# Grid attention by pairs of heads: score and value products on alternating halves of the array

## The chip, the cores and the metric

One core of one Trainium2 chip runs the whole kernel. The metric is the device time of one execution in microseconds (us); the kernel before takes 1773.36 us, the median of three runs (1773.16 to 1774.51).

In the rows, PE is the matrix engine (TensorE), PEld its loads of stationary operands, DVE is VectorE, ACT is ScalarE, POOL is GpSimd and SP is the queue that issues DMAs. "L879" is line 879 of the kernel.

## What is computed

One layer of a diffusion backbone: 512 latent tokens of 1024 channels, 256 context tokens. Three mixers (a gated convolution, a gated recurrence, a grid attention) run on one projection of the normalised tokens, are merged by gates and projected; a mixture of 16 experts follows. The change lies in the grid attention alone:

```python
def neighbourhood_attention(q, k, v, kc, vc, rpb):
...
        s_loc = jnp.einsum('bnqhd,bwnkhd->bhnqwk', qr, kr) * scale + bias[None]
        s_loc = jnp.where(in_win[:, :, None, :], s_loc, MASK_VALUE).reshape(...)
        s_ctx = jnp.einsum('bnqhd,blhd->bhnql', qr, kc) * scale
        p = jax.nn.softmax(jnp.concatenate([s_loc, s_ctx], axis=-1), axis=-1)
...
        o = jnp.einsum('bhnqwk,bwnkhd->bnqhd', p_loc, vr) + jnp.einsum('bhnql,blhd->bnqhd', p_ctx, vc)
```

There are 8 heads of width 64. The grid is 8 rows by 64 columns; a block of 16 columns (128 queries) sees 256 keys of the grid and all 256 context keys, so each softmax row has 512 entries.

## The kernel before

The first sub-layer is a stream of projections. Weights come in items of 1 MiB (`load_item`, L332); each is split into a high and a low part by `split_item` (L340): ScalarE casts a quarter (L353), VectorE subtracts it (L354), four quarters per item, spread over the first half of the steps of the item before. `proj` (L433) issues the products of one block of 128 channels: 8 steps of three 512-column matmuls (L440) into a bank `pj`.

Each engine runs its instructions in the order in which the program issues them. That order is written by `weave(fg, bg)` (L167): it issues the foreground steps `fg` one by one and puts the background pieces `bg` between them, evenly by cost. In the stage around the change (L1111) the foreground is the twelve projections of the convolution branch and four of the gates, 128 steps of three matmuls, and three small pieces that transpose the last value rows (`v_rows`, L840); the background is the grid attention.

The attention has 32 units, one per head and block of 16 columns. Two heads share a 128-row tile: head u = 0 lies on partitions 0 to 63, u = 1 on 64 to 127 of `nq`, `nk`, `nkc`. One background piece, `att_slot(n)` (L870), does one step of a pipeline that is four units deep:

- unit n: two score products (L879 grid keys, L880 context keys; 64 rows, 256 columns each) into a bank `hg`; VectorE adds the bias (L883) and takes the negated maximum (L884); ScalarE takes the exponential with the sum (L886);
- unit n − 1: VectorE takes the reciprocal of the sum (L890) and scales the row (L891);
- unit n − 3: four transposes (L896) into the bank `tp`, copied out by ScalarE (L898);
- unit n − 4: four value products (L910, stationary operand 64 columns wide, 128 columns streamed) into half of the partitions of a bank `acc`.

There are two `hg` banks, one `tp` bank, two `acc` banks and three `pj` banks. The operands of the attention are plain fp32, and the trace has two passes (a weight load and a matmul each) for every score and value product; transposes and the projections' matmuls have one. After the stage come the merge of the branches (L985), the output projection, the router and the experts, whose 384 MiB of weights stream through a ring of buffers (`ring_load`, L1017).

Of the kernel before, what the change touches and what calls it, by code (L numbers as in the profile page):

```python
# [10 lines left out]
F32 = mybir.dt.float32  # L11
F32R = mybir.dt.float32r
# [3 lines left out]
ALU = mybir.AluOpType  # L16
# [117 lines left out]
def mixer_moe(ctx: ExitStack, tc: tile.TileContext, a, out):  # L134
# [10 lines left out]
    def bank(tag):  # L145
        return psum.tile([128, 512], F32, tag=tag, name=tag, bufs=pbufs[tag])
# [8 lines left out]
    def g512(dt=F32):  # L155
        return gen.tile([128, 512], dt, tag="g", name="g", bufs=NA_)
# [23 lines left out]

# [1 line left out]
    xt = [[y512() for _ in range(2)] for _ in range(6)]  # L182
# [55 lines left out]

# [1 line left out]
    ssq = small([128, 6, 2], "ssq")  # L240
# [58 lines left out]

# [1 line left out]
    def mod_mm(pm, k, wm):  # L301
# [105 lines left out]

# [1 line left out]
    PASSES = ((0, 0), (0, 1), (1, 0))  # L409

    def use_item(n, blocks):
        """Steps of one streamed item, with the loads and splits of the next ones between them."""
        todo = split_item(n + 1)
        steps = []
        flat = [st for b in blocks for st in b]
        at = {int(p * len(flat) / 6): p for p in range(4)}
        for i, (c, f) in enumerate(flat):
            def g(i=i, f=f):
                if i == 0:
                    load_item(n + 1)  # L420
                    load_item(n + 2)
                f()
                if i in at and at[i] < len(todo):
                    todo[at[i]]()
            steps.append((c, g))
        return steps
# [6 lines left out]
    def proj(n, b, evac, with_ctx=False):  # L433
        """Channels of one block of columns over the tokens; the context follows LAG steps behind."""
        st = {}
# [23 lines left out]

# [1 line left out]
    slabs, mods = {}, {}  # L461
# [47 lines left out]

# [1 line left out]
    hv_t = per.tile([128, 8, 512], F32, tag="acc", name="hv", bufs=1)  # L511
# [33 lines left out]
    class Norms:  # L545
        """Norms over the head widths of several tiles at once: each head has a row of sums."""

# [3 lines left out]
        def sums(self, t, g, kind, cols=slice(0, 512)):  # L551
            """Sums of a tile's squares into row group g; kind 2 halves them, for twice the width."""
            def f():
                if not self.seen:
                    self.p = bank("acc")
                self.left -= 1
                PE.matmul(self.p[32 * g:32 * g + 32], zsel[kind], t(), start=(g not in self.seen), stop=(self.left == 0),
                          skip_group_check=True)
                self.seen.add(g)
            return f  # L560
# [33 lines left out]

# [1 line left out]
    def halves(t, m, lo=0, n=512):  # L596
# [200 lines left out]

# [1 line left out]
    perm_k = lambda t: t.rearrange("p (b r c) -> p r b c", b=8, r=8)  # L799
# [59 lines left out]

# [1 line left out]
    au = [(hp, cb, u) for hp in range(4) for cb in range(4) for u in range(2)]  # L861
    ast = {}
# [6 lines left out]

    def att_slot(n):  # L870
        def f():
            if n < 32:
                hp, cb, u = au[n]
                if n % 8 == 6 and hp < 3:
                    att_load(hp + 1)
                r = slice(64 * u, 64 * u + 64)
                qs = nq[hp][r, 128 * cb:128 * cb + 128]
                ps = bank("hg")
                PE.matmul(ps[:, 0:256], qs, nk[hp][r, 64 * KB0[cb]:64 * KB0[cb] + 256], start=True, stop=True)  # L879
                PE.matmul(ps[:, 256:512], qs, nkc[hp // 2][r, 256 * (hp % 2):256 * (hp % 2) + 256],  # L880
                          start=True, stop=True)
                st_ = gen.tile([128, 4], F32, tag="st", name="st", bufs=4)
                V.tensor_tensor(ps[:, 0:256], ps[:, 0:256], ast["b", hp, BTYPE[cb]][:, u], op=ALU.add)  # L883
                V.tensor_reduce(st_[:, 0:1], ps, axis=AX.X, op=ALU.max, negate=True)  # L884
                p = g512()
                S.activation(p, ps, AF.Exp, bias=st_[:, 0:1], accum_out=st_[:, 1:2])  # L886
                ast["p", n] = (p, st_)
            if 0 <= n - 1 < 32:
                p, st_ = ast["p", n - 1]
                V.reciprocal(st_[:, 2:3], st_[:, 1:2])  # L890
                V.tensor_scalar(p, p, st_[:, 2:3], None, op0=ALU.mult)  # L891
            if 0 <= n - 3 < 32:
                p, _ = ast.pop(("p", n - 3))
                pt = bank("tp")
                for c in range(4):
                    PE.transpose(pt[:, 128 * c:128 * c + 128], p[:, 128 * c:128 * c + 128], ident)  # L896
                pT = g512()
                S.copy(pT, pt)  # L898
                ast["t", n - 3] = pT
            if 0 <= n - 4 < 32:  # L900
                hp, cb, u = au[n - 4]
                pT = ast.pop(("t", n - 4))
                if (n - 4) % 8 == 0:
                    ast["o"] = bank("acc")
                po = ast["o"]
                vs = (nv["lat"][:, KB0[cb]], nv["lat"][:, KB0[cb] + 2], nv["ctx"][:, 0], nv["ctx"][:, 1])
                r = slice(64 * u, 64 * u + 64)
                hc = slice(128 * hp + 64 * u, 128 * hp + 64 * u + 64)
                for c in range(4):
                    PE.matmul(po[r, 128 * cb:128 * cb + 128], vs[c][:, hc], pT[:, 128 * c:128 * c + 128],  # L910
                              start=(c == 0), stop=(c == 3))
                if (n - 4) % 8 == 7:
                    hi, lo = g512(F32R), g512(F32R)
                    S.copy(nat_q(hi), perm_q(po))
                    V.tensor_tensor(nat_q(lo), perm_q(po), nat_q(hi.bitcast(F32)), op=ALU.subtract)
                    yv[2][hp] = (hi, lo)
        return f

# [1 line left out]
    cst = {}  # L920
# [24 lines left out]

# [1 line left out]
    mm = [None] * KT  # L947
# [53 lines left out]

# [1 line left out]
    chunks = []  # L1003
# [31 lines left out]

    # ==== the first sub-layer in program order ====
    for s in range(2):
# [21 lines left out]
    def insert(fg, ops):  # L1059
        """Puts (place, cost, function) between the steps of fg; returns it."""  # L1060
        res, ops = [], sorted(ops, key=lambda o: o[0])
        for i, st in enumerate(fg):
            while ops and ops[0][0] <= i:
                res.append(ops.pop(0)[1:])
            res.append(st)
        return res + [o[1:] for o in ops]
# [43 lines left out]
    fg = insert(fg, [(3 + n, 0.5, f) for n, f in enumerate(v_rows(3))])  # L1110
    weave(fg, [att_slot(n) for n in range(36)])  # L1111
    for n in range(4):
# [14 lines left out]

# [1 line left out]
    ga2, gb2 = mods["ga2"], mods["gb2"]  # L1129
# [94 lines left out]

# [1 line left out]
    wk = ctx.enter_context(tc.tile_pool(name="wk", bufs=2, side="right", reuse_waits="tile"))  # L1226
# [42 lines left out]
    def keep_warm(n):  # L1269
        """Products without a reader, so that the tensor engine's clock stays up while the selection runs."""  # L1270
        for _ in range(n):
            PE.matmul(pm, ident, xn[:, 0, 0:512], start=True, stop=True)
# [15 lines left out]

# [1 line left out]
    xps = {}  # L1290

    def chosen(pr):
        """Steps that gather a pair's rows of two channel tiles each."""
        def first():
# [25 lines left out]

# [1 line left out]
    used = [0]  # L1322
# [49 lines left out]
    def spread(e):  # L1372
        """Weights of an expert's slots over the tokens, slots on partitions, twice."""
        ow = wk.tile([128, 4, 2, CAP], F32, tag="s", name="ow")
# [27 lines left out]
    def down_half(e, h, r):  # L1402
        """The last expert goes by halves of the columns; its even and odd rows meet in the sum over the slots."""
        if r == 0:
# [69 lines left out]
```

## Time and profile before

| What | us |
|---|---|
| median of three runs | 1773.36 |
| span of the profiled execution (first to last instruction) | 1770.6 |
| what lies around the span, against the median | 2.8 |
| PE busy | 1667.7 (94%) |
| DVE busy | 572.1 (32%) |
| ACT busy | 367.7 (21%) |
| chain that ended last | PE 73%, DMA 11%, DVE 5% |

The profiled execution has no separate time beside the runs, so its own time is taken as its span and the 2.8 us around it. "Busy" is an average over stages with different limits: the projections keep PE full, and in the last third the chain also runs through DMAs of expert weights. What a change in one stage is worth has to be read in that stage.

### The profile page before, as it was taken

To read this page: it belongs to the slowest core of one execution; us is meant where nothing else is said; L and a number is where in the kernel's file an instruction comes from. 1 tells how busy PE (TensorE), PEld (TensorE's weight loads), DVE (VectorE), ACT (ScalarE), POOL (GpSimd) and SP (SyncE) were. 2 spreads that over 40 slices of the span, in tenths; PEclk is the share of its full clock that TensorE was granted. 3 is DMA by queue.
4 is the path that set the end of the run, shared out by engine and by line. 5 is a ranking of instruction groups with operands and counts; after the bars stand their busy time and mean duration, and the time that the engine had idled before them with its cause. 6 is when DMAs were issued, how large, how long until landed. Compare 5 with 4: busy or idle time off the path is not lost.

```text
span 1770.6 us, 20476 instructions
## 1 busy us (share of the span) xinstructions
PE 1667.7 (94%) x8382; PEld 949.9 (54%) x8382; DVE 572.1 (32%) x1135; ACT 367.7 (21%) x759; POOL 79.0 (4%) x150
## 2 busy tenths in 40 slices
PE   4999999999999999999999999998998998989988
PEld 2767888777777888896343343342432422424322
DVE  3518776435553443334011211121121121202111
ACT  4414445333334332223000010000000100000000
POOL 0214330000000000000000000000000000000000
PEclk8999999999999999999999999999999999999999
DMA  9860111111111233366999999999999999999997
GB/s 343 283 227 25 50 51 67 48 66 66 66 60 42 92 132 109 137 233 238 401 420 420 420 420 421 420 421 420 420 420 421 420 420 421 420 420 420 421 420 299
DMA packets 131690, 487.77 MB, mean 275 GB/s; under 512 B 8973, under 2 KB 12557, under 8 KB 125709
## 3 DMA queue, kind: packets, MB, share of 16 engines
q1 hardware_dynamic: 131596, 486.47, 69.2%
q8 instruction: 66, 1.08, 0.2%
q14 instruction: 28, 0.22, 0.0%
HBM read 484.34 MB, written 2.10 MB: 275 GB/s over the span
## 4 chain that ended last, share of the span: by engine, by line
PE 73%; DMA 11%; DVE 5%; ACT 1%; issue 1%; SPq 0%; DVEq 0%; ACTq 0%
PE pj L1343 19%; PE pj L440 19%; PE acc L1368 9%; PE hg L1397 5%; PE pj L985 4%; PE hg L1311 3%; PE pj L1175 2%; DMA B<-in_w_down_dram 2%; DMA D<-in_w_down_dram 2%; DMA W<-in_w_up_dram 2%; DMA B<-in_w_up_dram 2%; PE acc L910 2%; DVE acc L1400 2%; PE hg L879 1%; DMA A<-in_w_down_dram 1%; PE tp L896 1%
## 5 line engine op out<-in xcount | busy, mean ns | idle before, releaser
L440 PE MATMUL pj<-A,W 128*128 128x512 f32 x1536 | 400.8, 402 | 2.9 <-ACT W L353 1.9
L440 PEld LDWEIGHTS pj<-A,W 128*128 128x128 f32 x1536 | 276.4, 190 | 73.6 <-issue 20.1
L354 DVE TENSOR_TENSOR W<-W 128x512 fp32r<-128x512 f32 (+1 forms) x184 | 121.4, 686 | 155.4 <-ACT W L353 155.2
L1350 DVE TENSOR_TENSOR s<-s,pj 128x512 f32<-128x512 f32 x32 | 22.0, 688 | 453.7 <-PE pj L1343 367.0
L1343 PE MATMUL pj<-W,xe 128*64 128x512 f32 x688 | 156.5, 599 | 7.8 <-DMA W<-in_w_up_dram 4.4
L1348 ACT ACTIVATE s<-pj 128x512 f32<-128x512 f32 x32 | 19.1, 597 | 567.8 <-PE pj L1343 567.8
L1343 PE MATMUL pj<-A,xe 128*64 128x512 f32 x512 | 118.0, 605 | 5.2 <-DMA A<-in_w_gate_dram 4.2
L1397 PE MATMUL hg<-ye,oht 64*128 64x512 f32 x240 | 100.4, 683 | 16.5 <-DVE acc L1400 16.5
L1343 PEld LDWEIGHTS pj<-W,xe 128*64 128x64 f32 x688 | 47.4, 138 | 110.5 <-issue 86.4
L1343 PE MATMUL pj<-B,xe 128*64 128x512 f32 x432 | 98.5, 596 | 6.6 <-DMA B<-in_w_up_dram 4.4
L353 ACT CAST W<-W 128x512 fp32r<-128x512 f32 (+1 forms) x184 | 103.3, 600 | 0.0
L1400 DVE TENSOR_TENSOR acc<-acc,hg 128x512 f32<-128x512 f32 x120 | 77.7, 684 | 37.1 <-PE hg L1397 37.1
L1343 PEld LDWEIGHTS pj<-A,xe 128*64 128x64 f32 x512 | 35.2, 139 | 81.8 <-issue 66.3
L1397 PEld LDWEIGHTS hg<-ye,oht 64*128 64x128 f32 x240 | 32.7, 193 | 81.8 <-DVE acc L1400 69.6
L1389 DVE TENSOR_TENSOR ye<-mod,acc 64x512 f32<-64x512 f32 x30 | 20.6, 686 | 172.2 <-PE acc L1368 171.7
L1368 PE MATMUL acc<-W,at 128*64 128x512 f32 x320 | 71.7, 595 | 2.1 <-DMA W<-in_w_down_dram 2.1
L1343 PEld LDWEIGHTS pj<-B,xe 128*64 128x64 f32 x432 | 29.5, 137 | 70.0 <-issue 52.9
L1358 ACT COPY at<-tp 128x512 f32<-128x512 f32 x32 | 18.8, 586 | 219.1 <-PE tp L1356 218.6
L440 PEld LDWEIGHTS pj<-C,W 128*128 128x128 f32 x384 | 59.2, 190 | 9.2 <-ACT y L612 0.8
L440 PE MATMUL pj<-C,W 128*128 128x256 f32 x384 | 61.8, 283 | 0.0
L1311 PEld LDWEIGHTS hg<-ot,xn 128*128 128x128 f32 x512 | 57.9, 192 | 2.7 <-issue 2.7
L1311 PE MATMUL hg<-ot,xn 128*128 128x128 f32 x512 | 59.1, 276 | 0.2 <-DVE ot L1297 0.2
(289 smaller groups left out, 1875.1 us busy)
## 6 DMA issues: line engine op xcount, KB each, us to landing
W<-in_w_gate_dram SPq DMA_DIRECT2D x44, 1024.0 KB, 18.1
W<-in_w_up_dram SPq DMA_DIRECT2D x42, 1024.0 KB, 17.7
W<-in_w_down_dram SPq DMA_DIRECT2D x40, 1024.0 KB, 18.0
W<-in_w_in_dram SPq DMA_DIRECT2D x34, 1024.0 KB, 4.8
A<-in_w_gate_dram SPq DMA_DIRECT2D x34, 1024.0 KB, 18.1
B<-in_w_up_dram SPq DMA_DIRECT2D x34, 1024.0 KB, 17.5
B<-in_w_down_dram SPq DMA_DIRECT2D x31, 1024.0 KB, 18.1
A<-in_w_up_dram SPq DMA_DIRECT2D x30, 1024.0 KB, 17.9
```

The costliest lines, as they stand in the source:

```text
L353: S.copy(hi[:, sl], raws[n][:, sl])
L354: V.tensor_tensor(lo[:, sl], raws[n][:, sl], hi[:, sl].bitcast(F32), op=ALU.subtract)
L440: PE.matmul(dst, w[wi][:, k, 128 * b:128 * b + 128], src[xi][:, k], start=(k == 0 and p == 0), stop=(k == KT - 1 and p == 2))
L910: PE.matmul(po[r, 128 * cb:128 * cb + 128], vs[c][:, hc], pT[:, 128 * c:128 * c + 128], start=(c == 0), stop=(c == 3))
L985: PE.matmul(st["p"], wb[wi][:, 4 * br + k], yv[br][k][xi], start=(k == 0 and p == 0), stop=(k == 3 and p == 2))
L1175: PE.matmul(st["p"][:, 256 * u:256 * u + 256], mm[k][mi][:, ts], w[wi][:, k], start=(k == 0 and p == 0), stop=(k == KT - 1 and p == 2))
L1311: PE.matmul(px[:, 128 * k:128 * k + 128], xn[:, i, 128 * kk:128 * kk + 128], ot[:, 128 * i:128 * i + 128], start=(i == 0), stop=(i == 3))
L1343: PE.matmul(pg[64 * u:64 * u + 64], xp[:, kk, 64 * (e % 2):64 * (e % 2) + 64], wt[:, k, 512 * u:512 * u + 512], start=(kk == 0), stop=(kk ...
L1350: V.tensor_tensor(est["s", j], est["s", j], pg, op=ALU.mult)
L1368: PE.matmul(est["y"][64 * u:64 * u + 64], lhs, wt[:, k, 512 * u:512 * u + 512], start=(kk == 0), stop=(kk == 15))
L1397: PE.matmul(pc, oht[64 * u:64 * u + 64, 128 * i:128 * i + 128], ye[64 * u:64 * u + 64], start=True, stop=True)
L1400: V.tensor_tensor(av, av, pc, op=ALU.add)
```

## The change

A background piece no longer holds all four pipeline steps of one unit. The unit becomes a pair of heads (16 pairs), and each pair has four separate pieces, which `weave` spreads: `att_scores(n)`, the transposes of the first head of pair n − 1, the value products of pair n − 2, the transposes of the second head of pair n − 1. Scores are issued as key set by key set, head by head, so that neighbouring products use the two row halves of the array and the two `hg` banks; value products alternate between the two column halves and the two halves of `acc`'s partitions. The scaling (reciprocal and multiplication for both heads) is issued at the head of `att_turn(n, 0)`.

```diff
-    au = [(hp, cb, u) for hp in range(4) for cb in range(4) for u in range(2)]
+    au = [(hp, cb) for hp in range(4) for cb in range(4)]
...
+    def att_scores(n):
...
+            rs = [slice(64 * u, 64 * u + 64) for u in range(2)]
+            ps = [bank("hg") for _ in range(2)]
+            qs = nq[hp][:, 128 * cb:128 * cb + 128]
+            for c, keys in enumerate((nk[hp][:, 64 * KB0[cb]:64 * KB0[cb] + 256],
+                                      nkc[hp // 2][:, 256 * (hp % 2):256 * (hp % 2) + 256])):
+                for u in range(2):
+                    PE.matmul(ps[u][:, 256 * c:256 * c + 256], qs[rs[u]], keys[rs[u]], start=True, stop=True)
+            for u in range(2):
                 st_ = gen.tile([128, 4], F32, tag="st", name="st", bufs=4)
-                V.tensor_tensor(ps[:, 0:256], ps[:, 0:256], ast["b", hp, BTYPE[cb]][:, u], op=ALU.add)
-                V.tensor_reduce(st_[:, 0:1], ps, axis=AX.X, op=ALU.max, negate=True)
+                V.tensor_tensor(ps[u][:, 0:256], ps[u][:, 0:256], ast["b", hp, BTYPE[cb]][:, u], op=ALU.add)
+                V.tensor_reduce(st_[:, 0:1], ps[u], axis=AX.X, op=ALU.max, negate=True)
...
+    def att_scale(n):
+        for u in range(2):
+            p, st_ = ast["p", n, u]
+            V.reciprocal(st_[:, 2:3], st_[:, 1:2])
+            V.tensor_scalar(p, p, st_[:, 2:3], None, op0=ALU.mult)
+
+    def att_turn(n, u):
+        def f():
+            if u == 0:
+                att_scale(n)
+            p, _ = ast["p", n, u]
+            pt = bank("tp")
+            for c in range(4):
+                PE.transpose(pt[:, 128 * c:128 * c + 128], p[:, 128 * c:128 * c + 128], ident)
+            pT = g512()
+            S.copy(pT, pt)
...
+    def att_values(n):
...
+            for c in range(4):
+                for u in range(2):
+                    PE.matmul(po[64 * u:64 * u + 64, 128 * cb:128 * cb + 128],
+                              vs[c][:, 128 * hp + 64 * u:128 * hp + 64 * u + 64],
+                              pT[u][:, 128 * c:128 * c + 128], start=(c == 0), stop=(c == 3))
...
+    att_bg = []
+    for n in range(18):
+        att_bg += [att_scores(n) if n < 16 else None,
+                   att_turn(n - 1, 0) if 0 <= n - 1 < 16 else None,
+                   att_values(n - 2) if 0 <= n - 2 < 16 else None,
+                   att_turn(n - 1, 1) if 0 <= n - 1 < 16 else None]
...
-    weave(fg, [att_slot(n) for n in range(36)])
+    weave(fg, att_bg)
```

PE in the middle of the stage, before (`pj` is a projection's bank, `hg` the scores, `tp` the transposed rows, `acc` the output; `W`, `A` are weights and tokens, `nvl`, `nvc` values of grid and context):

```order
L440 MATMUL pj<-A,W 128x512 x9
L879 MATMUL hg<-g 128x256
L880 MATMUL hg<-g 128x256
L896 MATMUL tp<-ident,g 128x128 x4
L910 MATMUL acc<-g,nvl 64x128 x2
L910 MATMUL acc<-g,nvc 64x128 x2
L440 MATMUL pj<-A,W 128x512 x12
```

PE at the same place, changed:

```order
L881 MATMUL hg<-g 128x256 x4
L440 MATMUL pj<-A,W 128x512 x6
L904 MATMUL tp<-ident,g 128x128 x4
L440 MATMUL pj<-A,W 128x512 x6
L921 MATMUL acc<-g,nvl 64x128 x4
L921 MATMUL acc<-g,nvc 64x128 x4
L440 MATMUL pj<-A,W 128x512 x6
L904 MATMUL tp<-ident,g 128x128 x4
```

Scores of two heads stand together, value products of two heads too, and the transposes stand apart with projections before and behind them. Six projection matmuls lie between the scores of pair n and the first transposes of pair n − 1, in all 15 pairs that have both.

DVE, before, one unit and the start of the next (L883 and L884 bias and maximum, L890 and L891 the scaling, L354 the split of weights):

```order
L883 TENSOR_TENSOR hg<-hg,bias 128x256 [waits PE_49]
L884 TENSOR_REDUCE st<-hg 128x1 [waits DVE_49]
L890 RECIPROCAL st<-st 128x1
L891 TENSOR_SCALAR g<-g,st 128x512 [waits DVE_49]
L354 TENSOR_TENSOR W<-W 128x512 [waits Activation_49] x2
L883 TENSOR_TENSOR hg<-hg,bias 128x256 [waits DMAHW6_49,PE_49]
```

DVE, changed, the pair n = 5 (L884, L885 bias and maximum; L894, L895 the scaling):

```order
L884 TENSOR_TENSOR hg<-hg,bias 128x256 [waits DMAHW6_49,PE_49]
L885 TENSOR_REDUCE st<-hg 128x1 [waits DVE_49]
L884 TENSOR_TENSOR hg<-hg,bias 128x256 [waits PE_49]
L885 TENSOR_REDUCE st<-hg 128x1 [waits DVE_49]
L354 TENSOR_TENSOR W<-W 128x512 [waits Activation_49]
L894 RECIPROCAL st<-st 128x1
L895 TENSOR_SCALAR g<-g,st 128x512 [waits DVE_49]
L894 RECIPROCAL st<-st 128x1
L895 TENSOR_SCALAR g<-g,st 128x512 [waits DVE_49]
```

The scaling of pair n − 1 now stands behind the four score operations of pair n, and in this pair behind a split as well. Between the maxima and the scaling there is nothing in 7 of the 15 pairs; a split in n = 1, 5, 9, 11, 12, 14; the convolution's four operations and a split in n = 2; a gated product, its split and a weight split in n = 13.

ACT, changed, the same pair (L887 exponential, L353 cast of weights, L906 copy of transposed rows):

```order
L887 ACTIVATE g,st<-hg,st 128x512 [waits DVE_49,PE_49,Activation_49] x2
L353 CAST W<-W 128x512
L906 COPY g<-tp 128x512 [waits PE_49]
L541 CAST y<-g 128x512 [waits DVE_49]
L926 CAST g<-acc 128x512 [waits PE_49]
L353 CAST W<-W 128x512
L906 COPY g<-tp 128x512 [waits PE_49]
```

The cast that the split needs stands behind both exponentials of the pair; in n = 1 and n = 14 an evacuation of a projection (L946, L984) stands ahead of the cast too.

## Rows read from the trace of the kernel before

**Rows 1.** Busy time by stretch: us, busy (x instructions) by engine, granted clock, DMA share, GB/s

```profile
394.20:572.60 178.40, 178.40 (x894) 130.31 (x893) 90.92 (x186) 65.04 (x143) 0.00 (x0) 1.00 0.17 58
572.60:740.00 167.40, 167.40 (x735) 137.87 (x736) 63.67 (x104) 52.17 (x101) 9.00 (x7) 1.00 0.32 110
1215.00:1770.00 555.00, 503.76 (x2262) 179.25 (x2260) 96.25 (x174) 33.91 (x61) 0.00 (x0) 0.99 1.01 411
```

**Rows 2.** Timeline of PE, one unit: start, us, engine, line, operation, tile, count

```profile
441.60 0.70 PE L879 MATMUL hg<-g 64*128 64x256 f32 x2
442.14 0.59 PE L880 MATMUL hg<-g 64*128 64x256 f32 x2
442.66 0.66 PE L896 MATMUL tp<-ident,g 128*128 128x128 f32 x4
443.25 0.65 PE L910 MATMUL acc<-g,nvl 128*64 128x128 f32 x4
443.74 0.60 PE L910 MATMUL acc<-g,nvc 128*64 128x128 f32 x4
444.27 3.02 PE L440 MATMUL pj<-A,W 128*128 128x512 f32 x12
447.22 0.48 PE L879 MATMUL hg<-g 64*128 64x256 f32 x1
```

**Rows 3.** Chain of waits, runs of one kind of matmul: start, us, engine, tile, line

```profile
600.24 21.80 PE pj L440 x96
...
922.20 7.16 PE hg L1311 x64
...
938.22 13.73 PE pj L1343 x64
951.95 1.11 PE hg L1397 x4
```

**Rows 4.** Timeline of PE, transposes between projections

```profile
384.64 0.60 PE L849 MATMUL tp<-ident,g 128*128 128x128 f32 x4
385.00 0.71 PE L440 MATMUL pj<-A,W 128*128 128x512 f32 x2
```

**Rows 5.** Timeline of DVE, the same unit as rows 2

```profile
442.77 0.43 DVE L883 TENSOR_TENSOR hg<-hg,bias 128x256 f32<-128x256 f32 x1 [0.40 <-PE hg L880]
443.24 0.69 DVE L884 TENSOR_REDUCE st<-hg 128x1 f32<-128x512 f32 x1
443.84 0.15 DVE L890 RECIPROCAL st<-st 128x1 f32<-128x1 f32 x1
444.03 0.49 DVE L891 TENSOR_SCALAR g<-g,st 128x512 f32<-128x512 f32 x1
...
447.94 0.69 DVE L354 TENSOR_TENSOR W<-W 128x512 fp32r<-128x512 f32 x1
```

**Rows 6.** Timeline of ACT, the same unit

```profile
444.02 0.69 ACT L886 ACTIVATE g<-hg,st 128x512 f32<-128x512 f32 x1 [2.46 <-DVE st L890]
...
444.70 0.58 ACT L898 COPY g<-tp 128x512 f32<-128x512 f32 x1
...
447.21 0.61 ACT L353 CAST W<-W 128x512 fp32r<-128x512 f32 x1
```

**Rows 7.** Groups by line and shape, 394.2 to 572.6 us, the convolution on DVE

```profile
L935 DVE SCALAR_TENSOR_TENSOR g<-g,vecs 128x511 f32<-128x511 f32 x4 | 3.0, 752 | 0.1
```

**Rows 8.** Timeline of PE at two waits: in brackets the idle time and its releaser

```profile
56.55 0.74 PE L529 MATMUL pj<-W,A 128*128 128x256 f32 x4 [1.99 <-DVE W L354]
...
154.89 2.05 PE L711 MATMUL hg<-g 128*128 128x128 f32 x8 [3.12 <-DVE g L712]
```

**Rows 9.** Busy time of PE behind those two waits, granted clock before the DMA share

```profile
56.60:63.00 6.40, 4.77 (x38) 1.00 0.53 190
154.20:161.00 6.80, 6.11 (x23) 0.50 0.43 154
```

**Rows 10.** Line 867, loads of the bias

```profile
DMA to landing us min/median/max: 2.7/5.2/7.1
```

More of the change, by code (lines that the diff above doesn't have):

```diff
@@ L868, in att_load @@
             ast["b", hp, t] = b_
-    def att_slot(n):
+    def att_scores(n):
         def f():
[L872 to L881, printed above, removed]
+            hp, cb = au[n]
+            if cb == 3 and hp < 3:
+                att_load(hp + 1)
+            rs = [slice(64 * u, 64 * u + 64) for u in range(2)]
[6 more added lines that the diff above has]
+            for u in range(2):
@@ L882, in f @@
                 st_ = gen.tile([128, 4], F32, tag="st", name="st", bufs=4)
-                V.tensor_tensor(ps[:, 0:256], ps[:, 0:256], ast["b", hp, BTYPE[cb]][:, u], op=ALU.add)
-                V.tensor_reduce(st_[:, 0:1], ps, axis=AX.X, op=ALU.max, negate=True)
+                V.tensor_tensor(ps[u][:, 0:256], ps[u][:, 0:256], ast["b", hp, BTYPE[cb]][:, u], op=ALU.add)
+                V.tensor_reduce(st_[:, 0:1], ps[u], axis=AX.X, op=ALU.max, negate=True)
                 p = g512()
-                S.activation(p, ps, AF.Exp, bias=st_[:, 0:1], accum_out=st_[:, 1:2])
@@ L887, in f @@
[L887 to L916, printed above, removed]
@@ L917, in att_slot @@
-        return f
+                S.activation(p, ps[u], AF.Exp, bias=st_[:, 0:1], accum_out=st_[:, 1:2])
+                ast["p", n, u] = (p, st_)
+        return f
+    def att_scale(n):
[13 more added lines that the diff above has]
+            S.copy(pT, pt)
+            ast["t", n, u] = pT
+            del ast["p", n, u]
+        return f
@@ new lines, in att_values, with f @@
+    def att_values(n):
+        def f():
+            hp, cb = au[n]
+            pT = [ast.pop(("t", n, u)) for u in range(2)]
+            if cb == 0:
+                ast["o"] = bank("acc")
+            po = ast["o"]
+            vs = (nv["lat"][:, KB0[cb]], nv["lat"][:, KB0[cb] + 2], nv["ctx"][:, 0], nv["ctx"][:, 1])
+            for c in range(4):
[3 more added lines that the diff above has]
+                              pT[u][:, 128 * c:128 * c + 128], start=(c == 0), stop=(c == 3))
+            if cb == 3:
+                hi, lo = g512(F32R), g512(F32R)
+                S.copy(nat_q(hi), perm_q(po))
+                V.tensor_tensor(nat_q(lo), perm_q(po), nat_q(hi.bitcast(F32)), op=ALU.subtract)
+                yv[2][hp] = (hi, lo)
+        return f
@@ L920, in mixer_moe @@
+    att_bg = []
[4 more added lines that the diff above has]
+                   att_turn(n - 1, 1) if 0 <= n - 1 < 16 else None]
+    while att_bg[-1] is None:
+        att_bg.pop()
     cst = {}
```

## The prediction

> **What bounds the kernel now.** First the busy time by stretch [rows 1]. From 394.2 to 572.6 us, the stage that holds the attention, PE is busy for all of its 178.4 us; DVE for 91 and ACT for 65. So TensorE alone sets the length of this stage, and the two engines that evacuate have slack on average. The next stage, to 740 us, is all PE as well. Behind it the experts' weights stream at 411 GB/s, and the last third is bound by that stream; but the stream starts when the buffers of the first sub-layer come free, so a stage that ends x us earlier or later moves all behind it by x. I find nothing behind the stage that would absorb it, and count one for one.
>
> Then one unit on the timeline of PE [rows 2]. From its first score at 441.60 to the next unit's at 447.22 it takes 5.62 us, without an idle gap. A projection matmul in a long run costs 21.80 / 96 = 0.227 us [rows 3], so the twelve of this unit are 2.72 us and the attention's share is 2.90 us, 5.80 for two heads.
>
> Last the timelines of DVE and ACT over the same unit [rows 5, 6]: they give the steps between a score and the row that is ready to be transposed. Before, two whole units of PE work lie between the scaling of a row and its transposes, so these steps cost nothing. That is the cover to watch.
>
> **Part 1: less TensorE time.** A pass of 128 fp32 columns in the full array costs 7.16 / 64 = 0.112 us [rows 3], one of 256 columns then 0.224. A unit has four score passes (0.90), four transposes (0.45) and eight value passes (0.90): 2.24 us. The other 0.66 of its 2.90 us go to four changes of the array's shape (projection, scores, transposes, values, projection), 0.165 each.
>
> Do two halves run at once? The trace has both cases. The experts' L1343 alternates column halves: 64 passes of 512 columns in 13.73 us, 0.215 each, where 4 x 0.112 = 0.449 would be the price of one alone. L1397 alternates row halves, and where it doesn't wait for DVE, four passes of 512 columns take 1.11 us, not 4 x 0.449 = 1.80 [rows 3]. So I take half the price for both. A pair then has scores 0.90, values 0.90, eight transposes 0.90. Transposes have the shape of the projections and cost no change: four of them between projections take 385.00 - 384.64 = 0.36 us [rows 4]. So four changes are left per pair, 0.66. Sum 3.36 us against 5.80: **-2.44 us a pair, -39 us for 16**. The bound on this side is -36 (if the transposes' waits on semaphores cost 0.1 us each time) to -39.
>
> The Trainium skill speaks against the half of this: "TensorE: Matmul & The Clock Gate", Part 3, "The mechanism", says that weight loads overlap matmuls in flight only when the row group differs, which the column halves of the value products don't do. By that rule the values would save nothing, 16 x 0.90 = 14 us less, -25 in place of -39. The row of L1343 decides against it here.
>
> **Part 2: a new wait.** The scaling of pair n - 1 is issued with its first transposes. On PE six projection matmuls lie between the scores of pair n and these transposes; on DVE the scores' four operations lie before the scaling. Count from the moment when PE goes on behind the scores (442.66 in rows 2). PE arrives at the transposes after 6 x 0.227 plus half of the two changes around it (0.12): 1.48 us. On DVE [rows 5] the first bias addition starts at 0.11, its maximum 0.47 later, the next operation 0.60 after that: each head takes 1.07. So the reciprocal starts at 0.11 + 2 x 1.07 = 2.25, the multiplication 0.19 later, and it ends 0.49 after that, at 2.93. PE stands **1.45 us**. This holds in all 15 pairs that have both; in 7 nothing else lies between: 7 x 1.45 = 10 us.
>
> In eight pairs a weight split lies between, and its cast on ACT lies behind both exponentials. The second maximum starts at 1.65, the exponential 0.78 later (443.24 to 444.02), the next ACT operation 0.68 after that (444.02 to 444.70) [rows 5, 6]: the cast starts at 3.11. The subtraction starts 0.73 behind the cast's start (447.21 to 447.94) and takes 0.69, so the reciprocal waits until 4.53 and the multiplication ends at 5.21: a wait of **3.73 us**, in n = 5, 9, 11, 12. With an evacuation of 0.6 us ahead of the cast (n = 1, 14) 4.33. In n = 2 the convolution's four operations stand before the split; at 0.69, 0.49 and twice 0.75 [rows 7] they end at 4.93, the split at 5.62, the scaling at 6.30: 4.8. In n = 13 a gated product, its cast, its subtraction and the split bring it to some 5.9: 4.4. Together 4 x 3.73 + 2 x 4.33 + 4.8 + 4.4 = 33 us.
>
> Two smaller ones: behind the very first scores the copies that free `tp` for the last value rows stand behind both exponentials on ACT, about 2 us; and where the convolution's operations end just before the next scores, DVE begins these up to 1.8 us late, some 4 us over three pairs. Sum 10 + 33 + 2 + 4 = **+49 us**; 43 if DVE never lags, 56 if it lags twice as much and each wait has a tenth more of it in semaphores. In the rows of before the wait itself is not there; what is there are PE's waits for the same kinds of DVE work, 1.99 us for a split and 3.12 for a product [rows 8].
>
> **Part 3: the clock.** Behind the idle 3.12 us the granted clock is 0.50 (1.2 GHz) for 6.8 us, in which PE was busy for 6.11; behind the 1.99 us it stays at 1.00 [rows 8, 9]. At half clock 6.11 us hold the work of 3.05. All eight long waits are of 3.7 us or more, longer than the one that cost the clock, so I price each at 3.05: **+24 us**. Bounds: 0, if the clock holds, and 10 x 3.05 = 31 if two of the 1.45 us waits lower it too. The slow stretch ends before the next pair's wait, some 9 us later, so it takes nothing back there.
>
> **What costs nothing.** DVE and ACT do the same operations as before. Both `hg` banks are free when the next pair's scores come, since three pieces lie between. The loads of the bias are issued at the same place, a pair ahead of their first use; they land after 5.2 us (at most 7.1) [rows 10], and a pair takes longer. The cover here is the pair's length, and it grows. SP's queue issues the weight loads in the same order; POOL has nothing in this stage [rows 1].
>
> **Sum.** -39 + 49 + 24 = +34 us on 1770.6 + 2.8 = 1773.4, the median of the runs: **1807 us**. Bounds: -39 + 43 + 0 = +4 and -36 + 56 + 31 = +51.
>
> **Rivals.**
> - **The clock holds.** The waits are there but no stretch at 1.2 GHz follows: -39 + 49 = +10, 1783 us. For it speaks that 1.99 us of idle did no harm; against it that the waits are twice that and more. Chance 0.12.
> - **The value products don't overlap**, each half taking its full time because both halves load the same rows. +34 + 14 = +48, 1821 us. The row of L1343 speaks against it, where the same alternation has passes four times as long. Chance 0.07. It is what the rule of the Trainium skill's "TensorE: Matmul & The Clock Gate", Part 3, would give.
> - **The change doesn't do what it says**: neither kind of product overlaps, as the passes here are shorter (0.11 and 0.22 us) than in the rows with 512 columns. Then two times 14 us of saving are missing: +62, 1835 us. Chance 0.03.
> - **Faster: VectorE reaches the scaling early.** If the splits' casts are done before they are wanted, as they are on a ScalarE with slack (65 us of 178 [rows 1]), every wait is the short one: 15 x 1.45 = 22, no stretch at 1.2 GHz follows, and -39 + 22 = -17, 1756 us. It decides at a mean wait of 2.4 us a pair, 39 / 16. Against it speaks the order: the casts are issued behind the exponentials, and the engines keep to it. Chance 0.08.
>
> **The numbers.** My forecast has 0.70, with a range of its own from 1794 to 1824. To hold 8 in 10 I reach to the first rival below and to the second above: 1782 to 1832. About 0.2% (3.5 us) is what a measurement can tell from no change. Faster comes from the last rival, 0.08; within 0.2% only from the lowest corner of the sum, 0.02; slower 0.90.
>
> **What would show it.** Right: the scores' passes of a pair at twice the rate, value passes at half of 0.112 us; idle time of PE ahead of L904, released by DVE's L895, some 15 times 1.5 to 5 us; stretches at 0.50 in a stage that has none; the stage longer than 178.4 us by about 34, and all stages behind it as long as before. Wrong: no idle time ahead of L904, which would mean that I misread what stands between; or the passes of two halves one after the other; or a stage behind that shrinks as this one grows.

## The result and the profile after

The changed kernel takes **1801.09 us**, the median of four runs (1799.97 to 1802.37); the kernel before, run beside it, 1773.26 (four runs, 1771.73 to 1774.51). The ratio is 1.0163, with a 95% interval of 1.0148 to 1.0177: slower by 28 us. The prediction was 1807, in a range of 1782 to 1832.

In the changed kernel the scores stand on L881, bias and maximum on L884 and L885, the exponential on L887, the scaling on L894 and L895, the transposes on L904, the value products on L921; the merge of the branches, which begins the next stage, is L1006.

The page of the profile after, first busy time by engine, then the busy tenths and the granted clock in 40 slices of 45 us, then the chain:

```profile
span 1799.3 us, 20470 instructions
PE 1649.6 (92%) x8382; PEld 935.8 (52%) x8382; DVE 571.3 (32%) x1135; ACT 370.3 (21%) x759; POOL 80.2 (4%) x150
...
PE   4999999987877999999999999998998998989988
PEclk8999999998988999999999999999999999999999
...
PE 65%; DMA 16%; DVE 9%; ACT 2%; issue 1%; SPq 0%; ACTq 0%; DVEq 0%
...
L904 PE MATMUL tp<-ident,g 128*128 128x128 f32 x128 | 21.7, 296 | 43.9 <-DVE st L894 43.9
```

PE is busy for 18 us less than before (1667.7), in a span that is 28.7 us longer. The slices from 405 to 585 us, which lie in the stage of the attention, show sevens and an eight for PE and mostly eights for its clock. The group of the transposes, which waited for nothing before, has 43.9 us of idle PE ahead of it, all of it ended by VectorE's scaling. Now 9% of the chain are DVE's, where it was 5%.

The stage in figures. Windows of the kernel after: us, busy (instructions) of PE, PEld, DVE, ACT and POOL, granted clock, DMA share, GB/s. The first begins with the first score and ends before the first matmul of the merge; the second is the start of the next stage.

```profile
390.30:599.80 209.50, 163.51 (x900) 118.31 (x899) 90.68 (x187) 68.39 (x144) 0.00 (x0) 0.89 0.14 50
599.80:770.00 170.20, 170.20 (x749) 140.16 (x748) 65.18 (x107) 54.59 (x105) 9.01 (x7) 1.00 0.30 109
```

The same stretch of the kernel before, from the same moment (its own first score comes at 394.19) to its own merge, for PE alone:

```profile
390.30:572.50 182.20, 182.20 (x916) 1.00 0.16 57
```

So the stage takes 209.5 us in place of 182.2: **+27.3**, nearly all of the 28.7 us by which the span grew. Behind it PE is full at clock 1.00, as it was [rows 1]. The next window reads the stage's clock, at the nine stretches in which it stood at 0.50, the lower of its two levels (1.2 GHz); columns as before, PE alone:

```profile
395.46:398.87 3.41, 3.26 (x11) 0.50 0.00 0
405.70:412.53 6.83, 5.91 (x16) 0.50 0.63 230
419.35:426.18 6.83, 4.25 (x24) 0.50 0.02 5
456.90:460.31 3.41, 3.41 (x21) 0.50 0.00 0
...
569.54:576.37 6.83, 6.05 (x27) 0.50 0.43 156
sum 44.38, PE 39.27; mean PE 4.36
```

The four left out lasted 3.42, 6.82, 3.42 and 3.41 us. PE was busy for 39.27 us of the nine stretches. Taken as half speed, that is the work of 19.6 us. How near this is, the second of the stretches shows on the timeline of PE, in brackets the idle time and what ended it:

```profile
406.62 1.08 PE L904 MATMUL tp<-ident,g 128*128 128x128 f32 x4 [4.00 <-DVE st L894]
407.36 5.39 PE L440 MATMUL pj<-A,W 128*128 128x512 f32 x12
412.58 0.60 PE L904 MATMUL tp<-ident,g 128*128 128x128 f32 x4
```

Twelve projections take 5.22 us (407.36 to 412.58), 0.435 each, where one in a long run costs 0.227 [rows 3]: a little less than half of the time is lost, and 19.6 is an estimate that is some 4% high. With it, three numbers make up the stage: PE stands idle for 209.50 - 163.51 = **46.0 us**; the clock costs **19.6**; and what PE does would take 163.51 - 19.6 = 143.9 us at full clock where it took 182.2, **-38.3**. Together +27.3; the third number is what the other two leave.

Two pairs on the timeline of PE, one with a short wait and one with a long one. In brackets again the idle time and what ended it:

```profile
443.53 0.63 PE L904 MATMUL tp<-ident,g 128*128 128x128 f32 x4 [1.39 <-DVE st L894]
443.91 1.62 PE L440 MATMUL pj<-A,W 128*128 128x512 f32 x6
445.46 0.66 PE L921 MATMUL acc<-g,nvl 128*64 128x128 f32 x8
445.95 0.61 PE L921 MATMUL acc<-g,nvc 128*64 128x128 f32 x8
446.48 1.66 PE L440 MATMUL pj<-A,W 128*128 128x512 f32 x6
447.98 0.60 PE L904 MATMUL tp<-ident,g 128*128 128x128 f32 x4
448.33 1.64 PE L440 MATMUL pj<-A,W 128*128 128x512 f32 x6
449.90 1.13 PE L881 MATMUL hg<-g 64*128 64x256 f32 x8
450.97 1.67 PE L440 MATMUL pj<-A,W 128*128 128x512 f32 x6
456.16 0.63 PE L904 MATMUL tp<-ident,g 128*128 128x128 f32 x4 [3.52 <-DVE st L894]
```

What was bought is plain: the scores of two heads take 449.90 to 450.97, 1.07 us, where those of one took 1.06 [rows 2]; the value products of two heads 445.46 to 446.48, 1.02, where those of one took 1.02. What was paid stands in the brackets. Why the second wait is so long, the chain of waits of the kernel after tells, one step to a row in order of time (start, us, what):

```profile
449.97 1.11 PE hg L881 x8
451.09 0.42 DVE hg L884
...
451.54 0.69 DVE st L885
452.23 0.35 DVE hg L884
...
452.60 0.70 DVE st L885
...
453.41 0.78 ACT g L887 x2
454.19 0.52 ACT W L353
...
454.72 0.69 DVE W L354
455.42 0.09 DVE st L894
...
455.52 0.48 DVE g L895
456.01 0.08 DVE st L894
...
456.16 0.63 PE tp L904 x4
```

The row that is to be transposed belongs to the pair before; its exponential was done long ago. But VectorE first takes the two biases and maxima of the new scores, then the split of a weight (L354), and for that one ScalarE must finish the new pair's exponentials and the cast (L353). Only then come L894 and L895. Of the 5.2 us between the end of the scores and the transposes, PE has 1.67 us of projections to do.

### The profile page after: what moved, and what is told of

It reads as the page before. It is cut to its first block, busy times and chain, and to the rows that moved or that the text cites. A ratio compares the mean times of both kernels' runs of the same rounds, so it can differ in the third digit from the quotient of the medians.

```text
span 1799.3 us, 20470 instructions
## 1 busy us (share of the span) xinstructions
PE 1649.6 (92%) x8382; PEld 935.8 (52%) x8382; DVE 571.3 (32%) x1135; ACT 370.3 (21%) x759; POOL 80.2 (4%) x150
## 4 chain that ended last, share of the span: by engine, by line
PE 65%; DMA 16%; DVE 9%; ACT 2%; issue 1%; SPq 0%; ACTq 0%; DVEq 0%
PE pj L440 17%; PE pj L1364 16%; PE acc L1389 7%; PE hg L1418 5%; PE pj L1006 4%; PE hg L1332 3%; DMA W<-in_w_down_dram 3%; DMA B<-in_w_down_dram 3%; PE pj L1196 2%; DMA A<-in_w_down_dram 2%; DMA B<-in_w_up_dram 2%; DMA A<-in_w_up_dram 2%; DMA W<-in_w_up_dram 2%; DVE acc L1421 2%; DVE st L885 1%; PE acc L921 1%
## 5 line engine op out<-in xcount | busy, mean ns | idle before, releaser
L440 PE MATMUL pj<-A,W 128*128 128x512 f32 x1536 | 419.8, 413 | 2.9 <-ACT W L353 1.9
L440 PEld LDWEIGHTS pj<-A,W 128*128 128x128 f32 x1536 | 281.1, 194 | 75.8 <-issue 22.4
L354 DVE TENSOR_TENSOR W<-W 128x512 fp32r<-128x512 f32 (+1 forms) x184 | 122.1, 687 | 170.2 <-ACT W L353 169.9
L353 ACT CAST W<-W 128x512 fp32r<-128x512 f32 (+1 forms) x184 | 103.5, 599 | 0.0
L1421 DVE TENSOR_TENSOR acc<-acc,hg 128x512 f32<-128x512 f32 x120 | 77.4, 684 | 35.6 <-PE hg L1418 35.3
L904 PE MATMUL tp<-ident,g 128*128 128x128 f32 x128 | 21.7, 296 | 43.9 <-DVE st L894 43.9
## 6 DMA issues: line engine op xcount, KB each, us to landing
A<-in_w_up_dram SPq DMA_DIRECT2D x30, 1024.0 KB, 17.9
```

Source lines behind the costliest of these rows:

```text
L353: S.copy(hi[:, sl], raws[n][:, sl])
L354: V.tensor_tensor(lo[:, sl], raws[n][:, sl], hi[:, sl].bitcast(F32), op=ALU.subtract)
L440: PE.matmul(dst, w[wi][:, k, 128 * b:128 * b + 128], src[xi][:, k], start=(k == 0 and p == 0), stop=(k == KT - 1 and p == 2))
L1421: V.tensor_tensor(av, av, pc, op=ALU.add)
```

## The experiments

All runs change the kernel after. "The stage" is the time from the first score to the first matmul of the merge, or where named the moment of that matmul: 572.51 us in the kernel before, 599.84 in the kernel after. The kernel before is taken from the same moment on as the run that it is compared with. Ratios are against runs of the kernel before on the same chip.

### 1. The scaling ahead of the new scores' work

```diff
@@ att_scores(n), behind the eight score products
+            if n:
+                att_scale(n - 1)
             for u in range(2):
                 st_ = gen.tile([128, 4], F32, tag="st", name="st", bufs=4)
@@ att_turn(n, u)
-            if u == 0:
+            if u == 0 and n == 15:
                 att_scale(n)
```

> The changed kernel, with the scaling of pair n-1 issued ahead of the bias additions of pair n and no longer with the transposes; nothing else moves. Theory (the loss is PE's wait for the scaling, and the clock behind it): the waits ahead of the transposes vanish, no stretch at 0.50 is left in the stage, and what remains is the saving on TensorE, -39 us against the kernel before: about 1734 us, 1730 to 1740. Rival (VectorE and ScalarE have too much to do in this stage whatever the order): the wait comes back at the scores or at the copies, and the time stays above 1773 us.

Measured: 1743.68 us (1740.58 to 1746.47), ratio 0.9833 [0.9817, 0.9849]. The merge comes at 539.42, 33.1 us earlier than before and 60.4 earlier than in the kernel after. Windows of this kernel, PE alone, over the stage and over its only stretch at half clock:

```profile
390.20:539.40 149.20, 145.19 (x900) 0.99 0.20 70
395.54:398.95 3.41, 3.41 (x11) 0.50 0.00 0
```

The group of the transposes on its page:

```profile
L906 PE MATMUL tp<-ident,g 128*128 128x128 f32 x128 | 19.5, 274 | 1.9 <-DVE st L896 1.3 <-ACT g L908 0.6
```

Four instructions of VectorE for each pair, moved ahead of four others, take the 43.9 us of waiting for VectorE down to 1.9 (1.3 of them for VectorE), and eight of the nine slow stretches go with it. What is left of the idle time is 4.0 us, 2.14 of it at the very start of the stage; the one slow stretch behind that costs 1.7. So PE's own saving is 145.19 - 1.7 = 143.5 us against 182.3, -38.8: the first term, by itself. The run missed the expected time by 10 us in its median and 6 in its profiled execution (1740.58), and these some 6 are the 4.0 of idle and the 1.7 of clock that the expectation had left out; the other 4 of the median lie within the spread of its four runs.

### 2. The scaling behind the new scores' work, ahead of the splits

```diff
@@ att_scores(n), at its end, behind bias, maximum and exponential
+            if n:
+                att_scale(n - 1)
@@ att_turn(n, u)
-            if u == 0:
+            if u == 0 and n == 15:
                 att_scale(n)
```

> The changed kernel, with the scaling of pair n-1 issued right behind the maxima of pair n: behind the four score operations as in the change, but ahead of the weight splits and evacuations that stood between. Theory (a short wait of 1.5 us for the score operations, lengthened to 3.5 to 5 us in eight pairs by the split whose cast stands behind the exponentials): all fifteen waits are short, 15 x 1.5 = 23 us and about 2 us at the start, no stretch at 0.50 in the stage, -39 + 25 = -14: about 1759 us, 1754 to 1765. Rival (the casts are late for the projections too, so that the long waits only move to the projections): eight waits of 2 us or more remain, with a lower clock behind them, above 1775 us.

Measured: 1770.85 us (1766.46 to 1772.5, ten runs), ratio 0.9982 [0.9973, 0.9991]; the merge at 566.61, 5.9 us earlier than before. PE over the stage and over the longer of its two slow stretches:

```profile
390.40:566.60 176.20, 149.96 (x900) 0.97 0.17 59
505.33:512.16 6.83, 6.15 (x28) 0.50 0.30 100
```

One pair on the timeline of PE, behind its scores:

```profile
450.46 1.67 PE L440 MATMUL pj<-A,W 128*128 128x512 f32 x6
453.53 0.63 PE L906 MATMUL tp<-ident,g 128*128 128x128 f32 x4 [1.39 <-DVE st L896]
```

Nearly every pair now has the short wait, of 1.39 to 1.41 us, as no cast or split is issued between the scores and the scaling; three are longer, with 1.81, 2.93 and 2.34, as VectorE begins the new scores' work 0.44, 1.58 and 0.95 us late there. Idle time is 26.2 us in all, the clock costs (3.41 + 6.15) / 2 = 4.8, PE's own saving is the rest, -36.9. The expected 1754 to 1765 was too low: I had put the waits at 25 with the one at the start, not at 26, the clock at nothing and PE's saving at 39; and of the 5.9 us gained up to the merge the end of the span shows only 4.1. Why PE's saving is 2 us smaller here than in experiment 1 is not shown. What the rows offer is that a wait lets the matmul ahead of it run out: six projections take 1.67 us ahead of a wait, but 1.50 where the transposes follow at once (446.48 to 447.98 in the kernel after). The kernel after loses 46.0 + 19.6 = 65.6 us to idle time and clock, this one 31.0, experiment 1 5.7: so the four operations on VectorE ahead of the scaling cost some 25 of them, and what else was issued between, the splits above all, some 35.

### 3. The same order, the waits filled with matmuls

```diff
@@ att_turn(n, u), ahead of the transposes
             pt = bank("tp")
+            if u == 0 and n < 15:
+                for _ in range(14 if n + 1 in (1, 2, 5, 9, 11, 12, 13, 14) else 5):
+                    PE.matmul(pt, hT[0][:, 0, 0:128], hT[1][:, 0], start=True, stop=True)
             for c in range(4):
```

> The changed kernel, with matmuls that nobody reads (one pass of 512 columns, 0.23 us each) issued ahead of the first transposes of a pair, into the bank that the transposes overwrite: 5 in the pairs with a short wait, 14 in the eight with a long one, so that PE works instead of standing and arrives at the transposes no later than their rows. Theory (the waits cost 48 us and the low clock behind them another 20): the waits' length stays, the clock stays at 1.00, and the time falls by 15 to 20 us from 1801 to about 1783 us. Rival (the stage runs at the pace of VectorE and ScalarE, and the slow stretches cost nothing): 1801 us or a little more.

The added products are overwritten by the transposes. Measured: 1786.11 us (1785.01 to 1788.42), ratio 1.0076 [1.006, 1.0093]. The merge comes at 584.59: 12.1 us later than before, 15.2 earlier than in the kernel after (the stage itself is 17.0 us shorter, as it begins 1.8 us later). PE over the stage:

```profile
392.10:584.60 192.50, 181.44 (x1048) 0.99 0.16 54
```

And the long wait of the pair that was shown above, now filled (L905 are the fillers, L907 the transposes):

```profile
449.58 3.36 PE L905 MATMUL tp<-A 128*128 128x512 f32 x14
453.18 0.66 PE L907 MATMUL tp<-ident,g 128*128 128x128 f32 x4 [0.24 <-DVE g L895]
```

The 147 useless products of 0.227 us, 33 us of them, make the kernel 15 us faster. VectorE still issues the same things in the same order, and the time from the first score of a pair to its first transposes hardly changes (83.6 us over the 15 pairs, 84.6 in the kernel after). So what went is the price of the clock: one slow stretch is left of the nine, the one behind the 2.14 us at the start, ahead of all fillers. The stage's 17.0 us are near the 17.9 (19.6 less the 1.7 of that stretch) by which the clock was priced. That separates the two: the clock's price is real and follows from the idle time of PE, not from the attention's work.

### 4. Scores head by head

On top of experiment 1:

```diff
@@ att_scores(n)
-            for c, keys in enumerate((nk[hp][:, 64 * KB0[cb]:64 * KB0[cb] + 256],
-                                      nkc[hp // 2][:, 256 * (hp % 2):256 * (hp % 2) + 256])):
-                for u in range(2):
+            both = (nk[hp][:, 64 * KB0[cb]:64 * KB0[cb] + 256],
+                    nkc[hp // 2][:, 256 * (hp % 2):256 * (hp % 2) + 256])
+            for u in range(2):
+                for c, keys in enumerate(both):
                     PE.matmul(ps[u][:, 256 * c:256 * c + 256], qs[rs[u]], keys[rs[u]], start=True, stop=True)
```

> The kernel with the scaling first, with the score products issued head by head (both key sets of the first head, then both of the second) and no longer alternating; the products are the same. Theory (PE takes its matmuls in the order of issue, and two halves run together only where neighbours use different halves): of the four joint steps of a pair only the middle one is left, 8 passes take 7 steps of 0.216 in place of 4, 0.65 us a pair, about 10 us (14 if none is left): 1754 to 1758 us against 1744. Rival (PE lets the second half's passes overtake, so that pairing is enough): no difference, 1744 us.

Measured: 1743.85 us (1742.06 to 1746.44), ratio 0.9841 [0.9823, 0.9858], experiment 1's time; the stage takes 149.4 us, as there. My theory, that the halves must alternate to run together, falls. The timeline of PE has the same row for a pair's scores as with alternation (1.13 us); below it the same row, read only up to 452.65:

```profile
452.63 1.14 PE L882 MATMUL hg<-g 64*128 64x256 f32 x8
452.63 0.49 PE L882 MATMUL hg<-g 64*128 64x256 f32 x2
```

Two passes are under way at once; in single records the second starts 0.013 us after the first, where in the kernel before the second pass of one head starts 0.32 us behind its first. The rows name no head; I read the second as the first pass of the second head, though the program has three more passes of the first head between the two.

### 5. Value products head by head

On top of experiment 1:

```diff
@@ att_values(n)
-            for c in range(4):
-                for u in range(2):
+            for u in range(2):
+                for c in range(4):
                     PE.matmul(po[64 * u:64 * u + 64, 128 * cb:128 * cb + 128],
```

> The kernel with the scaling first, with the value products issued head by head and no longer alternating. Theory (overlap needs alternation): 16 passes take 15 or 16 steps of 0.109 us in place of 8, 0.76 to 0.87 us a pair, 12 to 14 us: 1756 to 1758 us against 1744. Rival (the queue finds the other half by itself): 1744 us. Other rival (the value products never gained anything from alternating): 1744 us too, told from the first by the passes' distances in the trace.

Measured: 1750.44 us (1747.75 to 1751.64), ratio 0.9872 [0.9854, 0.9889]: 6.8 us behind experiment 1, where 12 to 14 were expected; the stage takes 156.5 us against 149.2, +7.3. Timeline of PE, the value products of one pair (`nvl` are values of the grid, `nvc` of the context; each head has four passes on either):

```profile
451.12 0.65 PE L923 MATMUL acc<-g,nvl 128*64 128x128 f32 x4
451.61 0.27 PE L923 MATMUL acc<-g,nvc 128*64 128x128 f32 x1
451.61 0.32 PE L923 MATMUL acc<-g,nvl 128*64 128x128 f32 x1
451.71 0.27 PE L923 MATMUL acc<-g,nvc 128*64 128x128 f32 x1
451.77 0.27 PE L923 MATMUL acc<-g,nvl 128*64 128x128 f32 x1
...
452.10 0.60 PE L923 MATMUL acc<-g,nvc 128*64 128x128 f32 x4
452.63 1.67 PE L440 MATMUL pj<-A,W 128*128 128x512 f32 x6
```

The second head's `nvl` begin at 451.61 together with the first head's `nvc`, its fifth pass: four passes alone, four beside each other, four alone. That is 12 steps where alternation has 8, 1.51 us (451.12 to 452.63) in place of 1.02, and 16 times 0.49, 7.8 us, is about the loss. So here the order matters, but even so the halves run together for four of the steps. Neither the theory nor a rival had this.

### 6. Both head by head

Experiments 4 and 5 together.

> The kernel with the scaling first, with scores and value products both issued head by head: what is left of the change is that two heads share a piece and that transposes stand between projections, four changes of the array's shape per pair in place of eight. Theory (overlap is worth 28 us, the changes of shape 16 x 4 x 0.165 = 10.6): about 1744 + 22 to 28 = 1766 to 1772 us, still some 2 to 7 below the kernel before. Rival (most of the gain is the changes of shape): below 1755 us.

Measured: 1751.62 us (1748.68 to 1753.51), ratio 0.9882 [0.9866, 0.9897], stage 156.6 us: experiment 5 again. The time lies below the rival's 1755, but does not speak for the rival. The run was meant to leave only the saving in changes of shape, and it could not, since issuing head by head does not stop the halves from overlapping. So the split of the 38 us into overlap and changes of shape rests on rows alone; no run separates it.

### 7. The attention four steps later

On top of experiment 1, so that the copies for the last value rows (L851) no longer stand behind the first exponentials on ScalarE:

```diff
+    att_bg = [None] * 4 + att_bg
     weave(fg, att_bg)
```

> The kernel with the scaling first, with the attention's pieces starting four places later, so that the last value rows are transposed before the first scores. Theory: PE's wait of 2.1 us at the second of these transposes (for a copy that stood behind the exponentials) vanishes with the short stretch at 0.50 behind it, 3 to 4 us less than with the scaling first alone: about 1740 us. Rival (the wait is for something else, or comes back at the crowded end of the stage): no difference, or slower.

Measured: 1738.62 us (1737.48 to 1738.74), ratio 0.9808 [0.9793, 0.9824]. PE from 391.7, 3.4 us ahead of the first score, to the merge:

```profile
391.70:536.10 144.40, 142.16 (x892) 1.00 0.21 72
```

The wait at the start and its slow stretch are gone, the merge comes at 536.07, and no stretch of the stage is at half clock. This version is the best of all: 34.0 us less than the kernel before beside it (1772.61), 62.5 less than the kernel after, with the pairs of the change and the scaling in another place.

## Why the prediction was right, point by point

**The shape of it.** A saving on TensorE was given back by a wait on VectorE and by the clock behind it. All three are there, the first predicted within 1 us, the others each within 5: -39, +49 and +24 forecast, -38.3, +46.0 and +19.6 measured. The sum came out at 28 where 34 was said. That the stages behind it keep their length [rows 1] was right too: 27.3 of the 28.7 us of span arise in the stage, every stage down to the router comes 27.3 later, and the other 1.4 arise among the experts. One for one holds to 2 us: in experiments 1, 2 and 7 the merge comes 33.1, 5.9 and 36.4 us earlier, and the spans are shorter by 32.1, 4.1 and 35.3.

**Part 1.** Both kinds of products take one head's time for two. The sum is right; its split into overlap and changes of shape is not shown (experiment 6). The bound at -36 was not needed; experiments 1 and 7 have -38.8 and, by 142.16 us against the 180.8 from 391.7 to the merge of before, -38.6. Beside the measured 1.02 us for the values stands the rule of the Trainium skill, "TensorE: Matmul & The Clock Gate", Part 3, "The mechanism", that weight loads overlap matmuls in flight only when the row group differs. This trace disagrees, with sixteen passes on the same rows in the time that eight took, and with passes of the two halves that start 0.007 us apart. That column halves would save nothing by this rule was the prediction's inference; the section does not say it.

**Part 2.** The order on VectorE gave the waits almost to the number: seven short ones of 1.39 to 1.42 us (1.45 was said, 9.8 us in all against 10), eight long ones between 3.52 and 5.06 (33.8 us against 33), and 2.14 at the start (2). Two sizes were off, and what they make together hides it: the long waits are only 0.8 us above their sum. The last item, "where the convolution's operations end just before the next scores, DVE begins these up to 1.8 us late, some 4 us over three pairs", came out at 2.9: VectorE begins 0.44, 1.58 and 0.96 us behind the scores' end in n = 9, 11 and 12, where 0.03 is usual. Without that lag the eight long waits sum to 30.9 and not to 33; the plain ones (n = 5, 9, 11, 12) are 3.5 us, where 3.73 was said. Experiments 1 and 2 show that the place of the scaling is the cause: ahead of the four operations 1.3 us are left of it, behind them but ahead of the splits the short wait alone.

**Part 3.** The step that failed in its size is "All eight long waits are of 3.7 us or more, longer than the one that cost the clock, so I price each at 3.05". There were nine slow stretches, one with each long wait and one with the 2.14 us at the start; by [rows 8, 9] I had expected a wait of about 2 us to do no harm. And five of the nine lasted 3.4 us and not 6.8, so that each cost some 1.7. Together 19.6 in place of 24. That this came so near is in part luck: the price was read off a single wait, and without the ninth stretch, which was not foreseen, it would be 18.0. Experiment 3 shows it as a cost by itself.

**The rivals.** The clock did not hold, both products overlap, and the change does what it says. The faster one had its mechanism wrong at the root: casts are not early, VectorE and ScalarE keep to the order in which the program issues. Experiment 2 gives every pair about the wait that this rival assumed and still comes out only 3 us ahead of before, not 17, since the waits of the pairs still sum to 24 us where it had 22, the start adds its 2.1, two slow stretches cost 4.8, PE's saving is 2 us smaller, and 1.8 us of the gain are lost among the experts.

## What to carry to other kernels

Pairing two products on the halves of the array is worth what the rows say, here 2.4 us a pair; but a piece that is cut out of a pipeline must take its place in every engine's order, not in TensorE's alone. Ask of each operation that TensorE will wait for: what is issued ahead of it on its own engine, and does any of that wait for work that has only just begun? Here the scaling needed nothing that was new and stood behind four operations that did, in eight of fifteen pairs also behind a split whose cast stood behind the new exponentials. Moving it ahead of them turned +28 us into -30, and a later start of the attention made that -34.

## What was not expected of the hardware

- **TensorE starts passes of another half ahead of passes issued before them.** Scores of a second head start 0.013 us behind the first head's first pass, with three issued in between, as I read the rows (experiment 4); of the values the second head starts beside the first head's fifth pass, not its second (experiment 5). The same section of the Trainium skill that was named above has matmuls start and end strictly in the order of the program; the starts recorded here do not bear that out for products on different halves. So "each engine runs its instructions in the order in which the program issues them", as said ahead of the prediction, is too strong for TensorE.
- **Useless work can save time.** 33 us of extra matmuls took 15 us off the kernel, as they kept the granted clock at 1.00 in eight of the nine stretches in which it had stood at 0.50 (experiment 3).
- **What lowers the clock was not a plain matter of one wait's length.** Behind 2.14 us of idle it fell to 0.50 (after, experiment 1), behind 1.99 us in the kernel before it did not [rows 8, 9]; in experiment 2 it fell behind 2.14 and 2.93 us and held behind 2.34; and behind none of the seven waits of 1.4 us did it fall. The slow stretches lasted 3.4 or 6.8 us. In the kernel after those of 6.8 us all began while PE still stood, 0.7 to 2.6 us ahead of the wait's end (405.70 and 406.62 in the rows above); those of 3.4 us began between 0.15 us ahead of it and 1.0 us behind it (456.90 and 456.16). Why, no run here tells.
